# Two-input operations of GpSimd over more than 256 columns, issued in two halves

## The chip, the cores and the metric

The kernel runs on one core of a Trainium2 chip. Five engines work side by side, each through its own instructions in a fixed order: TensorE (PE; its weight loads are shown apart as PEld), VectorE (DVE), ScalarE (ACT), GpSimd (POOL) and SyncE (SP), which here issues the DMA transfers. They wait for each other through semaphores. The metric is the time of one execution on the device in microseconds (us). Three runs of the kernel before took 1324.07 to 1325.41 us, with a median of 1325.01 us.

## What is computed

One layer of a streaming encoder, for 2048 new frames with 16 meta tokens in front (the prompt) and for 32 new frames of a running stream with a cache of 528 rows (the sample). All numbers are float32. In short form:

```
n  = rmsnorm(x, norm_g)
q, k, v, z_a, b, c, u, z_c = split(n @ w_in, 8)          # 8 parts of 512 columns
# group A: differential attention, 4 heads, q and k in two halves of 64
s1, s2 = q1 k1 / 8 + bias, q2 k2 / 8 + bias              # chunk-causal, chunks of 64 frames
o  = (softmax(s1) - lam * softmax(s2)) @ v
o  = rmsnorm_per_head(o, subln_g) * 0.8 * silu(z_a)
# group B: gated short convolution
y  = silu(z_c) * b * conv3(c * u)                        # depthwise, causal, width 3
x  = x + concat(o, y) @ w_out
out = rmsnorm(x, final_g)
```

The outputs are the normalised rows of the prompt and the sample, the new keys and values, and the last two rows of the convolution's input.

## The kernel before

**Products in three parts.** TensorE multiplies in a reduced-precision form of float32. So each factor is split into a high part, rounded by a copy to that form, and a low part, the difference between the number and its high part. A product is the sum of high x high, high x low and low x high. The high parts are made by ScalarE (`S.copy`), the low parts by a subtraction with two inputs, which for the most part GpSimd does (`G.tensor_tensor(..., op=ALU.subtract)`) and for some tensors VectorE.

**Stages.** The prompt is worked on in four parts p of 512 frames; the first also carries the 16 meta tokens and the 32 sample frames, 560 columns in all. For each p, x is read transposed (`x_load`), scaled by norm_g and split into `xh` and `xl`; the normalising factor of each frame is kept in `rbs[p]` and applied to the results. For each of the four heads h follow:

- `unit_a(h, p)`: the projections q, k, v and z. `w_load` brings the 128 columns of one projection (`wr`), and splits them into `wh` and `wl` in two pieces of 4 x 128 columns (L196, L197). `proj` multiplies (L217): 24 matmuls for each block of 512 columns, or of 280, 272 or 288 for p = 0. The blocks are read out by VectorE with two inputs, PSUM and `rbs`. The low parts of q and k are made by GpSimd on 64 partitions (L252, L278), that of v on 128 (L313).
- `attend(h, p, st)`: for each row tile of 128 frames `softmax_diff` computes the scores of both halves in chunks of up to 512 columns (L438, L439), VectorE takes each row's extremum (L385, L388), and ScalarE the exponential (L389). `coefs` works out a few numbers per row on VectorE and ScalarE (L358 to L369), and each chunk is then combined by GpSimd, which scales the first half with one input (`G.tensor_scalar`, L392), and by VectorE, which adds the second half with two inputs (L393). TensorE transposes the result (L454), it is split again (L457, L458) and multiplied with v (L461 to L463). `post` normalises and gates it; its last product is GpSimd's (L422).
- `unit_c(u, p)`: the projections c, u, b and the gate with the convolution between them. GpSimd does three products here (L532, L554, L568).

Behind the four parts comes the output projection (`out_first`, `out_rest`), whose rows are split by `load_cat` (L664, L666) and whose weights by `w_half` (L649, L650), with matmuls at L686.

**The order of the work.** The program is written as loops, but the order of instructions on each engine is set by a scheduler, which simulates the engines with costs of its own as the kernel is built and takes what is ready by priority (`schedule_with_timeline_sim=True`). So the matmuls of one projection stand between those of another unit's attention. Where the code changes, the order is worked out again for all engines.

Of the kernel before, what the change touches and what calls it, by code (L numbers as in the profile page):

```python
# [13 lines left out]
AF = mybir.ActivationFunctionType  # L14
ALU = mybir.AluOpType
# [21 lines left out]
CQ, CK, CV, CZ, CB, CC, CU, CG = range(0, 32, 4)  # L37
# [10 lines left out]
def hybrid_step(ctx: ExitStack, tc: tile.TileContext, x, xT, ckT, cv, scT, rel_bias, norm_g, w_in,  # L48
# [10 lines left out]
    op = pool("op", 3)  # L59
# [9 lines left out]
    V, S, G, T = nc.vector, nc.scalar, nc.gpsimd, nc.tensor  # L69
    S.preload_act_table_set("natural_log_exp_and_others")  # L70
    f32 = lambda a: a.bitcast(F32) if a.dtype == F32R else a
    dma = lambda out, in_: nc.sync.dma_start(f32(out), f32(in_))
    g_tile = lambda n=564: gp.tile([P, 564], F32, tag="g", name="g")[:, :n]
    o_tile = lambda n=QT: op.tile([P, QT], F32, tag="o", name="o")[:, :n]
# [23 lines left out]
    rbs = {}  # L98
# [34 lines left out]
    def x_load(p):  # L133
        c0 = 0 if p == 0 else NX + QT * p
        tw = NX + QT if p == 0 else QT
        if p == 0:
            acc = [None, None]
        for k in range(KT):
            xt = g_tile(tw) if p == 0 else one.tile([P, QT], F32, tag="xt", name="xt", bufs=XB)
            dma(xt, xT[P * k:P * (k + 1), c0:c0 + tw])  # L140
            xh[k] = xp.tile([P, NX + QT], F32R, tag=f"xh{k}", name=f"xh{k}")
            xl[k] = xp.tile([P, NX + QT], F32R, tag=f"xl{k}", name=f"xl{k}")
            with tc.high_priority():
                S.activation(xh[k][:, :tw], xt, AF.Copy, scale=ng[:, k:k + 1])
                V.scalar_tensor_tensor(xl[k][:, :tw], xt, ng[:, k:k + 1], f32(xh[k][:, :tw]),  # L145
                                       op0=ALU.mult, op1=ALU.subtract)
            if p == 0:
                i = (1, 0, 1, 0, 1, 0, 0, 0)[k]
                sq = sqt(k, tw)
                (G.tensor_tensor(sq, xt, xt, op=ALU.mult) if i else S.activation(sq, xt, AF.Square))  # L150
                if acc[i] is None:
                    acc[i] = sq
                else:
                    (G if i else V).tensor_tensor(acc[i], acc[i], sq, op=ALU.add)
        if p == 0:
            rb = one.tile([P, NX + QT], F32, tag="rb", name="rb")
            for i in range(2):
                c = slice(280 * i, 280 * (i + 1))
                var, w = (pp.tile([P, 512], F32, tag="p1", name="xv", bufs=NP[1])[:, :280] for _ in range(2))
                ps = ps_t.tile([P, 2, 256], F32, tag="pt", name="pss").rearrange("p a b -> p (a b)")[:, :280]  # L160
                parts = [a[:, c] for a in acc if a is not None]
                for j, a in enumerate(parts):
                    T.matmul(ps, lhsT=ones, rhs=a, start=(j == 0), stop=(j == len(parts) - 1))
                with tc.high_priority():
                    rsqrt(rb[:, c], ps, var, w, 1.0 / D)
            rbs[0] = rb
# [21 lines left out]
    def w_load(col, p):  # L188
        wr = wp.tile([P, KT, P], F32, tag="wraw", name="wr")
        dma(wr, w_in[col])  # L190
        w2 = []
        for i in range(2):
            wh = wp.tile([P, KT // 2, P], F32R, tag="wh", name="wh", bufs=4)
            wl = wp.tile([P, KT // 2, P], F32R, tag="wl", name="wl", bufs=4)
            wi = wr[:, KT // 2 * i:KT // 2 * (i + 1)]
            S.copy(wh, wi)  # L196
            (V if (col in (CQ, CK) if p == 0 else col in (CQ, CZ)) else G).tensor_tensor(wl, wi, f32(wh), op=ALU.subtract)  # L197
            w2.append((wh, wl))
        return w2

# [28 lines left out]
    def unit_a(h, p):  # L229
# [8 lines left out]
        q32 = g_tile(tw)  # L238
# [6 lines left out]
        def ev_q(ps, b0, b1):  # L245
            V.scalar_tensor_tensor(q32[:, b0:b1], ps, -0.125, rbs[p][:, b0:b1], op0=ALU.mult, op1=ALU.mult)
            e = min(b1, f0 + QT)
            for c in range(2):
                r = slice(64 * c, 64 * c + 64)
                hi, lo = (t_[r, b0 - f0:e - f0] for t_ in qd[c])  # L250
                S.copy(hi, q32[r, b0:e])
                G.tensor_tensor(lo, q32[r, b0:e], f32(hi), op=ALU.subtract)  # L252
            if p == 0 and b1 == tw:
                for c in range(2):
                    V.tensor_copy(qs[64 * c:64 * c + 64, NS * c:NS * (c + 1)], q32[64 * c:64 * c + 64, smp])
        proj(CQ + h, p, ev_q)
        for c in range(2):
            r, o = slice(64 * c, 64 * c + 64), slice(64 - 64 * c, 128 - 64 * c)
# [6 lines left out]
        k32 = g_tile(tw)  # L265
        ks = [ks_tile(c) for c in range(2)]
# [4 lines left out]
        def ev_k(ps, b0, b1):  # L271
            V.tensor_tensor(k32[:, b0:b1], ps, rbs[p][:, b0:b1], op=ALU.mult)
            e = min(b1, kn)
            for c in range(2):
                r, o = slice(64 * c, 64 * c + 64), slice(64 - 64 * c, 128 - 64 * c)
                d = slice(k0 + b0, k0 + e)
                S.copy(ks[c][r, d], k32[r, b0:e])
                G.tensor_tensor(ks[c][o, d], k32[r, b0:e], f32(ks[c][r, d]), op=ALU.subtract)  # L278
        proj(CK + h, p, ev_k)
        dma(kT_p[h, :, k0:k0 + kn], k32[:, :kn])  # L280
        if p < NQ - 1:
# [17 lines left out]
        vh = kv.tile([P, 16, P], F32R, tag="vh", name="vh")  # L299
        vl = kv.tile([P, 16, P], F32R, tag="vl", name="vl")  # L300
# [9 lines left out]
        v32 = v32.rearrange("p (j d) -> p j d", d=P)  # L310
        S.copy(v32, pt)
        V.tensor_copy(vh[:, new], v32)
        G.tensor_tensor(vl[:, new], v32, f32(vh[:, new]), op=ALU.subtract)  # L313
        r0 = NM + QT * p
        dma(v_p[r0:r0 + QT, h].rearrange("(j q) d -> q j d", q=P), v32)
        if p < NQ - 1:
# [92 lines left out]
    def post(n, o32, sq, z, l1, dst):  # L409
        sqh, sql = (ap.tile([P, 2, 256], F32R, tag=t_, name="sqh").rearrange("p a b -> p (a b)")[:, :n]  # L410
                    for t_ in ("ah", "al"))
        V.tensor_copy(sqh, sq)
        V.tensor_tensor(sql, sq, f32(sqh), op=ALU.subtract)
        ps = ps_o.tile([P, 512], F32, tag="po", name="pss")[:, :n]
        T.matmul(ps, lhsT=ones_r, rhs=sqh, start=True, stop=False)
        T.matmul(ps, lhsT=ones_r, rhs=sql, start=False, stop=True)
        f = o_tile(n)
        S.activation(f, ps, AF.Ln, scale=1.0 / P, bias=leps[:, 0:1])
        V.scalar_tensor_tensor(f, f, 0.5, l1, op0=ALU.mult, op1=ALU.add)
        S.activation(f, f, AF.Exp, scale=-1.0)  # L420
        V.scalar_tensor_tensor(o32, o32, g2[:, 0:1], f, op0=ALU.mult, op1=ALU.mult)
        G.tensor_tensor(o32, o32, z, op=ALU.mult)  # L422
        dma(dst, by_tile(o32) if n == QT else o32)

    def attend(h, p, st):
# [93 lines left out]
    def unit_c(u, p):  # L519
# [9 lines left out]

        def ev_c(ps, b0, b1):  # L530
            V.tensor_tensor(c32[:, b0:b1], ps, rbs[p][:, b0:b1], op=ALU.mult)
            G.tensor_tensor(c32[:, b0:b1], c32[:, b0:b1], rbs[p][:, b0:b1], op=ALU.mult)  # L532
        proj(CC + u, p, ev_c)

        def spans(b0, b1):
# [15 lines left out]

        t4 = g_tile(tw)
        for s0, s1, off in spans(f0, tw):
            G.tensor_tensor(yc[:, s0 + off - 2:s1 + off - 2], yc[:, s0 + off - 2:s1 + off - 2], rbs[p][:, s0:s1],  # L554
                            op=ALU.mult)

        def ev_b(ps, b0, b1):
            for s0, s1, off in spans(b0, b1):
# [4 lines left out]
        def ev_g(ps, b0, b1):  # L563
            eb = e[:, b0:b1]
            V.tensor_tensor(zc[:, b0:b1], ps, rbs[p][:, b0:b1], op=ALU.mult)
            softplus_neg(eb, zc[:, b0:b1])
            S.activation(eb, eb, AF.Exp, scale=-1.0)
            G.tensor_tensor(zc[:, b0:b1], zc[:, b0:b1], t4[:, b0:b1], op=ALU.mult)  # L568
        proj(CG + u, p, ev_g)
        V.tensor_tensor(t4[:, f0:], zc[:, f0:], e[:, f0:], op=ALU.mult)  # L570
        dma(cat[p][:, :, 4 + u], by_tile(t4[:, f0:hn]))
# [81 lines left out]
    def load_cat(t, rows, spare=False):  # L653
        ct = wp.tile([P, KT, P], F32, tag="wraw", name="ct")
        dma(ct[:, :, :rows], cat_s if t == 16 else cat[t // 4][:, t % 4])
        parts = []
        for i in range(2):
            c = ct[:, 4 * i:4 * i + 4, :rows]
            if spare:
                chh, cll = [pp.tile([P, 4, P], F32R, tag="p0", name="cs", bufs=NP[0]) for _ in range(2)]  # L660
            else:
                chh = wp.tile([P, 4, P], F32R, tag="wh", name="chh", bufs=4)
                cll = wp.tile([P, 4, P], F32R, tag="wl", name="cll", bufs=4) if t < 16 else chh
            S.copy(chh[:, :, :rows], c)  # L664
            lo = cll[:, :, :rows] if t < 16 else cll[:, :, rows:2 * rows]
            (V if spare or t == 16 else G).tensor_tensor(lo, c, f32(chh[:, :, :rows]), op=ALU.subtract)  # L666
            parts.append((chh, cll))
        hi, lo = ([parts[k // 4][j][:, k % 4] for k in range(KT)] for j in range(2))
        return hi, lo if t < 16 else None
# [136 lines left out]
```

## Time and profile before

| | |
|---|---|
| runs before | 1324.07 to 1325.41 us, median 1325.01 us |
| the profiled execution | 1324.97 us, span 1323.2 us |
| TensorE busy | 1279.3 us, 97% of the span |
| VectorE busy | 1011.5 us, 76%, 2086 instructions |
| ScalarE busy | 738.0 us, 56% |
| GpSimd busy | 731.3 us, 55%, 659 instructions |
| granted TensorE clock, mean | 0.990 |

The span reaches from the first to the last instruction of the profiled execution. An engine counts as busy while one of its instructions runs, standing still inside an instruction included. L197 is line 197 of the kernel before. A row of a group gives line, engine, operation, written and read tiles, shape, count, then the busy time in us and the mean of one in ns, then the idle time of the engine just before these instructions and what ended it. A row of waits gives who waited for whom, the us in total, how often, and the longest. A row of the timeline gives start and length in us, and in brackets the idle time before.

### The profile page before, as it was taken

Reading aid. Unit: us, or ns where it says so; the run is one execution under the profiler, and the core shown is the slowest. Engines: PE = TensorE matmul, PEld = TensorE weight load, DVE = VectorE, ACT = ScalarE, POOL = GpSimd, SP = SyncE. Lnnn points to the kernel's source line nnn. Section 1 sums busy time; section 2 is a strip of 40 time slices with the busy share of each in tenths; the row PEclk is TensorE's granted clock in tenths of the full one; section 3 lists DMA queues with packets and bytes.
Section 4 is the critical chain, followed back from the end, with each engine's and each line's share of the span. In section 5 each row is a group of like instructions: output and inputs, shape, how many; then the busy total and the mean of one; then the engine's idle time right before and its main releaser. Section 6 shows DMA issues by size and latency. Waiting matters only on the chain.

```text
span 1323.2 us, 21113 instructions
## 1 busy us (share of the span) xinstructions
PE 1279.3 (97%) x7058; PEld 1102.2 (83%) x7058; DVE 1011.5 (76%) x2086; ACT 738.0 (56%) x1854; POOL 731.3 (55%) x659
## 2 busy tenths in 40 slices
PE   8999999999999998999999999999999999999997
PEld 6999899988788886888888788888888887888775
DVE  8766567668797857788878868888798898856754
ACT  6645453664665547566565466565656665654322
POOL 4665655656566664466556656466666575642200
PEclk9999999999999999899999999999999999999999
DMA  9744434674335356534253463344334534557752
GB/s 285 219 141 108 138 99 113 205 243 145 121 105 174 106 159 192 169 127 151 96 168 102 135 194 100 124 131 124 105 104 153 161 110 128 159 183 231 231 176 90
DMA packets 108046, 198.72 MB, mean 150 GB/s; under 512 B 17409, under 2 KB 45601, under 8 KB 107937
## 3 DMA queue, kind: packets, MB, share of 16 engines
q1 hardware_dynamic: 107936, 197.37, 48.4%
q8 instruction: 55, 0.90, 0.3%
q14 instruction: 55, 0.44, 0.1%
HBM read 145.62 MB, written 43.26 MB: 143 GB/s over the span
## 4 chain that ended last, share of the span: by engine, by line
PE 30%; DVE 12%; ACT 3%; issue 2%; POOL 2%; DMA 1%; DVEq 0%; POOLq 0%; ACTq 0%
PE po L686 10%; PE pj L217 10%; DVE p L393 4%; PE pt L454 2%; PE s L438 2%; DVE nm L388 2%; PE s L439 2%; ACT p L389 1%; PE po L462 1%; PE po L463 1%; PE po L461 1%; DVE al L458 1%; POOL wl L197 1%; PE po L678 1%; DMA out<-y 0%
## 5 line engine op out<-in xcount | busy, mean ns | idle before, releaser
L217 PE MATMUL pj<-xh,wh 128*128 128x512 f32 (+2 forms) x1280 | 457.0, 358 | 3.8 <-DVE g L344 1.0
L217 PE MATMUL pj<-xl,wh 128*128 128x512 f32 (+2 forms) x1280 | 455.2, 356 | 1.7 <-DVE xl L145 1.7
L197 POOL TENSOR_TENSOR wl<-wr,wh 128x512 fp32r<-128x512 f32 x240 | 327.7, 1370 | 232.5 <-ACT wh L196 220.6
L217 PE MATMUL pj<-xh,wl 128*128 128x512 f32 (+2 forms) x1280 | 453.5, 355 | 0.0
L389 ACT ACTIVATE p<-s,nm 128x384 f32<-128x384 f32 (+5 forms) x352 | 208.6, 595 | 164.5 <-DVE nm L388 126.0
L217 PEld LDWEIGHTS pj<-xh,wh 128*128 128x128 f32 x1280 | 243.3, 190 | 35.4 <-ACT bvec L596 1.7
L217 PEld LDWEIGHTS pj<-xl,wh 128*128 128x128 f32 x1280 | 242.9, 190 | 30.9 <-DVE xl L145 3.2
L217 PEld LDWEIGHTS pj<-xh,wl 128*128 128x128 f32 x1280 | 242.8, 190 | 30.0 <-issue 1.1
L196 ACT CAST wh<-wr 128x512 fp32r<-128x512 f32 x256 | 157.1, 617 | 99.6 <-PE pj L217 61.4
L393 DVE SCALAR_TENSOR_TENSOR p<-p,cf,p 128x384 f32<-128x384 f32 (+5 forms) x176 | 176.6, 1025 | 21.9 <-POOL p L392 21.2
L392 POOL TENSOR_SCALAR p<-p,cf 128x384 f32<-128x384 f32 (+5 forms) x176 | 122.1, 709 | 60.6 <-DVE cf L369 42.1
L438 PE MATMUL s<-ks,q 128*128 128x384 f32 (+5 forms) x352 | 130.1, 371 | 12.0 <-ACT p L389 11.8
L388 DVE TENSOR_REDUCE nm<-s 128x1 f32<-128x384 f32 (+3 forms) x224 | 121.8, 557 | 2.8 <-PE s L439 2.6
L439 PE MATMUL s<-ks,q 128*128 128x384 f32 (+5 forms) x352 | 123.7, 352 | 0.0
L458 DVE TENSOR_TENSOR al<-pt,ah 128x512 fp32r<-128x512 f32 x144 | 97.0, 681 | 34.6 <-ACT ah L457 34.5
L666 POOL TENSOR_TENSOR cll<-ct,chh 128x512 fp32r<-128x512 f32 x40 | 55.9, 1404 | 108.6 <-ACT chh L664 108.6
L457 ACT CAST ah<-pt 128x512 fp32r<-128x512 f32 x144 | 80.8, 586 | 39.1 <-PE pt L454 36.7
L454 PE MATMUL pt<-ident,p 128*128 128x128 f32 x544 | 88.4, 274 | 1.6 <-DVE p L393 1.4
L438 PEld LDWEIGHTS s<-ks,q 128*128 128x128 f32 x352 | 66.7, 189 | 25.8 <-ACT p L389 18.7
L462 PE MATMUL po<-al,vh 128*128 128x256 f32 x288 | 83.5, 290 | 2.1 <-DVE al L458 2.0
L461 PE MATMUL po<-ah,vh 128*128 128x256 f32 x288 | 81.3, 282 | 0.0
L463 PE MATMUL po<-ah,vl 128*128 128x256 f32 x288 | 81.2, 282 | 0.0
(238 smaller groups left out, 2214.4 us busy)
## 6 DMA issues: line engine op xcount, KB each, us to landing
wr<-in_w_in SPq DMA_DIRECT2D x128, 512.0 KB, 3.7
ct<-cat SPq DMA_DIRECT2D x28, 512.0 KB, 4.6
q<-q SPq DMA_DIRECT2D x64, 128.0 KB, 2.8
out<-y SPq DMA_DIRECT2D x32, 256.0 KB, 3.7
ks<-ksd SPq DMA_DIRECT2D x8, 776.0 KB, 5.2
xr<-in_x SPq DMA_DIRECT2D x24, 256.0 KB, 5.3
out<-g SPq DMA_DIRECT2D x24, 256.0 KB, 2.9
xt<-in_xT SPq DMA_DIRECT2D x24, 256.0 KB, 4.7
```

The costliest lines, as they stand in the source:

```text
L196: S.copy(wh, wi)
L197: (V if (col in (CQ, CK) if p == 0 else col in (CQ, CZ)) else G).tensor_tensor(wl, wi, f32(wh), op=ALU.subtract)
L217: T.matmul(ps, lhsT=a[:, k % 4], rhs=b[k][:, b0:b1], start=(k == 0 and i == 0), stop=(k == KT - 1 and i == 2))
L388: V.tensor_reduce(nm[:, c, j:j + 1], s, op=ALU.min, axis=AX.X)
L389: S.activation(pr[j][c], s, AF.Exp, bias=nm[:, c, j:j + 1], scale=-1.0, accum_out=l[:, c, j:j + 1])
L392: G.tensor_scalar(a0, a0, cf[:, 0, j:j + 1], 1.0, op0=ALU.mult, op1=ALU.mult)
L393: V.scalar_tensor_tensor(a0, a1, cf[:, 1, j:j + 1], a0, op0=ALU.mult, op1=ALU.add)
L438: T.matmul(ps, lhsT=qd[c][0][:, qs], rhs=ks[c][:, col:col + w], start=True, stop=False)
L439: T.matmul(ps, lhsT=qd[c][1][:, qs], rhs=ks[c][:, col:col + w], start=False, stop=True)
L454: T.transpose(pt[:, i, P * qi:P * (qi + 1)], cols(aa[qi], NM + P * (2 * j + i), P), ident)
L458: V.tensor_tensor(al, pt, f32(ah), op=ALU.subtract)
L686: T.matmul(ps, lhsT=a[k][:, :rows], rhs=b[k], start=(k == 0 and i == 0), stop=(k == KT - 1 and i == 2))
```

## The change

A function `halved` takes the place of `tensor_tensor` at ten places. Where the engine is GpSimd and the operation covers more than 256 columns (counted over all dimensions behind the partitions), it issues two instructions, one for each half of the first of these dimensions; otherwise one, as before. For VectorE, where a condition chooses it at L197 and L666, nothing changes. The operations with one input (L392), those of 32, 240 and 248 columns, and those of L154 and L650 stay as they are. 435 operations become 870 instructions.

```diff
+    def halved(out, a, b, op, engine=None):
+
+        n = out.shape[-1] if len(out.shape) == 2 else out.shape[1]
+        cuts = (0, n // 2, n) if engine is None and n * (out.shape[-1] if len(out.shape) > 2 else 1) > 256 else (0, n)
+        for c0, c1 in zip(cuts, cuts[1:]):
+            (engine or G).tensor_tensor(out[:, c0:c1], a[:, c0:c1], b[:, c0:c1], op=op)
...
-                (G.tensor_tensor(sq, xt, xt, op=ALU.mult) if i else S.activation(sq, xt, AF.Square))
+                (halved(sq, xt, xt, ALU.mult) if i else S.activation(sq, xt, AF.Square))
...
-            (V if (col in (CQ, CK) if p == 0 else col in (CQ, CZ)) else G).tensor_tensor(wl, wi, f32(wh), op=ALU.subtract)
+            halved(wl, wi, f32(wh), ALU.subtract, V if (col in (CQ, CK) if p == 0 else col in (CQ, CZ)) else None)
...
-                G.tensor_tensor(lo, q32[r, b0:e], f32(hi), op=ALU.subtract)
+                halved(lo, q32[r, b0:e], f32(hi), ALU.subtract)
...
-                G.tensor_tensor(ks[c][o, d], k32[r, b0:e], f32(ks[c][r, d]), op=ALU.subtract)
+                halved(ks[c][o, d], k32[r, b0:e], f32(ks[c][r, d]), ALU.subtract)
...
-        G.tensor_tensor(vl[:, new], v32, f32(vh[:, new]), op=ALU.subtract)
+        halved(vl[:, new], v32, f32(vh[:, new]), ALU.subtract)
...
-        G.tensor_tensor(o32, o32, z, op=ALU.mult)
+        halved(o32, o32, z, ALU.mult)
...
-            G.tensor_tensor(c32[:, b0:b1], c32[:, b0:b1], rbs[p][:, b0:b1], op=ALU.mult)
+            halved(c32[:, b0:b1], c32[:, b0:b1], rbs[p][:, b0:b1], ALU.mult)
...
-            G.tensor_tensor(yc[:, s0 + off - 2:s1 + off - 2], yc[:, s0 + off - 2:s1 + off - 2], rbs[p][:, s0:s1],
-                            op=ALU.mult)
+            halved(yc[:, s0 + off - 2:s1 + off - 2], yc[:, s0 + off - 2:s1 + off - 2], rbs[p][:, s0:s1], ALU.mult)
...
-            G.tensor_tensor(zc[:, b0:b1], zc[:, b0:b1], t4[:, b0:b1], op=ALU.mult)
+            halved(zc[:, b0:b1], zc[:, b0:b1], t4[:, b0:b1], ALU.mult)
...
-            (V if spare or t == 16 else G).tensor_tensor(lo, c, f32(chh[:, :, :rows]), op=ALU.subtract)
+            halved(lo, c, f32(chh[:, :, :rows]), ALU.subtract, V if spare or t == 16 else None)
```

The change also moves instructions. GpSimd, in the first head's attention (p = 0, h = 0), with `p` the tiles of the softmax chunks, `wl` a weight's low part and `g<-g,rb` the product at L532; first the order before, then the order of the change, whose line 78 is inside `halved` and whose L400 is the L392 of before:

```order
L392 TENSOR_SCALAR p_685<-p_685,cf 128x272
L197 TENSOR_TENSOR wl<-wr,wh 128x512
L392 TENSOR_SCALAR p_730<-p_730,cf 128x400
L532 TENSOR_TENSOR g<-g,rb 128x280
L197 TENSOR_TENSOR wl<-wr,wh 128x512
```

```order
L400 TENSOR_SCALAR p_697<-p_697,cf 128x272
L78 TENSOR_TENSOR wl<-wr,wh 128x256 x2
L78 TENSOR_TENSOR g<-g,rb 128x140 x2
L78 TENSOR_TENSOR wl<-wr,wh 128x256 x2
L400 TENSOR_SCALAR p_742<-p_742,cf 128x400
```

Each pair of halves stands together, with nothing of another kind between, and the scaling of the chunk of 400 columns now follows the product of L532 and another weight's low part. VectorE at the same place (`x` and `nm` are small tiles with a few numbers per row, ISA is L385's operation, `al` and `am` low parts), before and with the change, where L401 is L393, L396 is L388 and L393 is L385:

```order
L388 TENSOR_REDUCE nm<-s 128x1
L393 SCALAR_TENSOR_TENSOR p_730<-p_731,cf,p_730 128x400
L388 TENSOR_REDUCE nm<-s 128x1
L109 TENSOR_REDUCE x_2406<-ssq 128x4
L170 TENSOR_SCALAR x_2407<-x_2406 128x4
L385 ISA s,nm<-s,bz 128x256
L385 ISA nm 128x1
L458 TENSOR_TENSOR al<-pt,ah 128x512
L469 TENSOR_TENSOR am_116<-pm,am_116 16x256
```

```order
L396 TENSOR_REDUCE nm<-s 128x1
L181 TENSOR_TENSOR x_2475<-x_2474 128x4
L182 TENSOR_TENSOR x_2475<-x_2475,x_2473 128x4
L393 ISA s,nm<-s,bz 128x256
L393 ISA nm 128x1
L183 TENSOR_SCALAR x_2475<-x_2475 128x4
L466 TENSOR_TENSOR al<-pt,ah 128x512
L184 TENSOR_TENSOR x_2474<-x_2474,x_2475 128x4
L477 TENSOR_TENSOR am_116<-pm,am_116 16x256
L401 SCALAR_TENSOR_TENSOR p_742<-p_743,cf,p_742 128x400
```

The combining of the chunk of 400 columns stood between the two minima of L388; with the change it follows both of them, the small operations on `x`, one extremum with the bias, and the two splits `al` and `am`.

## The prediction

> **What bounds the kernel now.** I read the page first: its busy shares and its chain.
>
> ```profile
> span 1323.2 us, 21113 instructions
> PE 1279.3 (97%) x7058; PEld 1102.2 (83%) x7058; DVE 1011.5 (76%) x2086; ACT 738.0 (56%) x1854; POOL 731.3 (55%) x659
> PE 30%; DVE 12%; ACT 3%; issue 2%; POOL 2%; DMA 1%; DVEq 0%; POOLq 0%; ACTq 0%
> ```
>
> TensorE is busy 97% of the span, and the engine that the change touches is on 2% of the followed chain. So the question is what the remaining 43.9 us of TensorE idle time (1323.2 - 1279.3) are, and whether GpSimd has a hand in them. The busy time by stretch tells where they lie:
>
> ```profile
> 0.00:20.00 20.00, 14.18 (x48) 10.00 (x49) 14.59 (x24) 13.09 (x22) 9.28 (x16) 1.00 0.83 242
> 20.00:130.00 110.00, 109.26 (x832) 105.08 (x831) 79.13 (x216) 61.39 (x167) 68.07 (x71) 1.00 0.61 182
> 130.00:340.00 210.00, 201.98 (x1310) 182.62 (x1309) 144.53 (x314) 108.15 (x277) 125.24 (x117) 0.99 0.52 155
> 340.00:540.00 200.00, 192.49 (x957) 161.87 (x957) 155.25 (x329) 116.83 (x290) 119.35 (x103) 0.97 0.48 151
> 540.00:740.00 200.00, 196.71 (x1055) 169.20 (x1053) 170.26 (x348) 121.75 (x311) 117.06 (x105) 1.00 0.41 131
> 740.00:1040.00 300.00, 296.25 (x1553) 252.43 (x1552) 246.79 (x457) 182.27 (x439) 182.98 (x159) 1.00 0.43 129
> 1040.00:1180.00 140.00, 136.33 (x721) 115.69 (x720) 119.13 (x210) 86.93 (x221) 87.06 (x73) 1.00 0.45 145
> 1180.00:1300.00 120.00, 116.51 (x530) 92.96 (x530) 71.39 (x164) 42.90 (x115) 22.22 (x17) 0.99 0.65 207
> 1300.00:1323.20 23.20, 15.59 (x68) 12.33 (x66) 10.44 (x30) 4.72 (x16) 0.00 (x0) 0.90 0.14 51
> ```
>
> The columns are the stretch, its length, the busy time of TensorE, of its weight load, VectorE, ScalarE and GpSimd, then the granted clock. The first and last rows hold 5.8 and 7.6 us of idle TensorE (first loads, last output), which the change can't reach. The seven between them hold 30.5 us in all. Three of these also show a granted clock below 1.00: 1% of 210, 3% of 200 and 1% of 120 us, some 9 us of full clock lost. That is all there is to win: about 40 us. Then who ends these waits:
>
> ```profile
> PE s L438 <- ACT p L389: 11.8, 11, 3.3
> PE ptv L308 <- DVE g L297: 4.0, 3, 1.7
> PE pts L504 <- DVE as L499: 2.9, 2, 2.2
> PE po L462 <- DVE al L458: 2.0, 2, 1.3
> ```
>
> They are score matmuls waiting for a score tile to be read out (ScalarE's exponential at L389, which itself waits for VectorE's minimum at L388), or direct waits for VectorE. No row of this view names GpSimd. But GpSimd is behind VectorE's lateness in another way, which two pieces of the timeline show. Columns: start, length, engine, line. GpSimd, then VectorE:
>
> ```profile
> 656.47 1.61 POOL L568 TENSOR_TENSOR g<-g 128x512 f32<-128x512 f32 x1
> 658.04 1.74 POOL L197 TENSOR_TENSOR wl<-wr,wh 128x512 fp32r<-128x512 f32 x1
> 668.60 1.29 POOL L197 TENSOR_TENSOR wl<-wr,wh 128x512 fp32r<-128x512 f32 x1
> ```
>
> ```profile
> 656.85 1.78 DVE L419 SCALAR_TENSOR_TENSOR o<-o,g 128x512 f32<-128x512 f32 x1
> 668.80 1.11 DVE L363 TENSOR_TENSOR nm<-nm,M 128x8 f32<-128x8 f32 x1 [0.64 <-ACT p L389]
> ```
>
> L363 handles 8 columns and took 1.11 us: it began at 668.80, inside GpSimd's L197, and ended at 669.91, just after that instruction (669.89). L419 began inside L568, was still running when L568 ended at 658.08, and ended at 658.63; the next GpSimd instruction, already queued, took 1.74 instead of 1.29 us, longer by 0.45, about VectorE's turn. So a VectorE operation that needs what GpSimd holds stands still **until the end of GpSimd's whole instruction**, and gets its turn there, ahead of the next one. How much of that there is, from the groups by shape:
>
> ```profile
> L393 DVE SCALAR_TENSOR_TENSOR p<-p,cf,p 128x384 f32<-128x384 f32 x64 | 69.2, 1103 | 0.0
> L393 DVE SCALAR_TENSOR_TENSOR p<-p,cf,p 128x400 f32<-128x400 f32 x44 | 42.2, 958 | 14.2 <-POOL p L392 14.0
> L393 DVE SCALAR_TENSOR_TENSOR p<-p,cf,p 128x512 f32<-128x512 f32 x44 | 50.8, 1161 | 0.0
> L368 DVE TENSOR_TENSOR r<-r,lam 128x2 f32<-128x2 f32 x52 | 22.2, 427 | 1.4
> L367 DVE RECIPROCAL r<-M 128x2 f32<-128x2 f32 x52 | 8.5, 164 | 1.5
> ```
>
> ```profile
> 531.78 0.63 DVE L393 SCALAR_TENSOR_TENSOR p<-p,cf,p 128x400 f32<-128x400 f32 x1
> 661.19 0.73 DVE L393 SCALAR_TENSOR_TENSOR p<-p,cf,p 128x512 f32<-128x512 f32 x1
> ```
>
> Undisturbed, L393 takes 0.63 us at 400 columns and 0.73 at 512, by the line through these 0.615 at 384. Its three groups are longer by 64 x 0.49 + 44 x 0.33 + 44 x 0.43 = 65 us. L368, on the same two columns as L367 but with two inputs, is longer by 52 x 0.263 = 14 us. Doing the same for every VectorE instruction against the shortest tenth of its shape gives some 224 us standing: 203 us in 272 instructions behind GpSimd's two-input ones, 0.75 us each, and 21 us behind L392, which has one. A fifth of VectorE's 1011.5 busy us is this.
>
> The largest idle stretch of TensorE shows the link. TensorE, VectorE and GpSimd before it:
>
> ```profile
> 524.61 0.40 PE L217 MATMUL pj<-xh,wl 128*128 128x512 f32 x1
> 528.28 0.59 PE L438 MATMUL s<-ks,q 128*128 128x272 f32 x1 [3.28 <-ACT p L389]
> ```
>
> ```profile
> 523.85 1.24 DVE L363 TENSOR_TENSOR nm<-nm,M 128x4 f32<-128x4 f32 x1
> 525.61 1.22 DVE L173 TENSOR_TENSOR x<-x 128x4 f32<-128x4 f32 x1
> 526.95 0.57 DVE L388 TENSOR_REDUCE nm<-s 128x1 f32<-128x400 f32 x1
> ```
>
> ```profile
> 523.69 3.12 POOL L278 TENSOR_TENSOR ks<-g,ks 64x512 fp32r<-64x512 f32 x2 [0.19 <-ACT ks L277]
> 526.89 1.27 POOL L197 TENSOR_TENSOR wl<-wr,wh 128x512 fp32r<-128x512 f32 x1
> ```
>
> Two operations on four columns take 1.24 and 1.22 us behind the two instructions of L278, and the minimum at 526.95 that frees the score tile stands behind them. In the 6 us before the 33 TensorE gaps of over 0.2 us VectorE stood still 2.2 us in the mean, against 0.93 us in any 6 us (203 / 1310 x 6).
>
> **The change, part by part.** *Length of a half.* GpSimd's two-input operations by width:
>
> ```profile
> L197 POOL TENSOR_TENSOR wl<-wr,wh 128x512 fp32r<-128x512 f32 x240 | 327.7, 1370 | 232.5 <-ACT wh L196 220.6 <-PE pj L217 3.6 <-PE s L439 2.1
> L278 POOL TENSOR_TENSOR ks<-g,ks 64x280 fp32r<-64x280 f32 x8 | 6.2, 781 | 1.6 <-ACT ks L277 1.1
> L554 POOL TENSOR_TENSOR g<-g,rb 128x32 f32<-128x32 f32 x4 | 1.0, 243 | 0.0
> ```
>
> From 243 ns at 32 and 781 at 280 columns: 2.17 ns a column and 174 ns an instruction. This gives 1.28 us at 512 (the undisturbed 1.29 above) and 0.73 us at 256. Two halves are 1.46 us, 0.17 more. The lower bound is 0.13, since a following instruction starts some 0.04 us before its predecessor ends (658.04 against 658.08); the upper one 0.25, from the mean 1370 at 512 against 781 at 280, which has the waits in it. I take 0.17, the undisturbed rows. 435 operations are split (240 in L197, 40 in L666, 155 in the others), so GpSimd gets 435 x 0.17 = 74 us more, bounds 57 and 109: 55% busy becomes 61%. The cover is GpSimd's own idle time, 592 us, of which 220.6 before L197 wait for ScalarE's copy. If that cover fails, it is the slower rival below.
>
> *The standing of VectorE.* If VectorE gets its turn between halves, it waits for the rest of 0.73 instead of 1.29 us. 0.75 x 0.73 / 1.29 = 0.42 us; with GpSimd busier by a tenth about 300 such meetings, 127 us in place of 203. So VectorE wins some 75 us, and the bounds are 0 (no turn between the halves) and 100 (half of it). The 21 us behind L392 stay, since it isn't split.
>
> *From VectorE to TensorE.* VectorE runs ahead of or behind TensorE with idle time of its own; only what falls before the 30.5 us of gaps counts. If of the 2.2 us before each gap 45% go, and no gap shrinks by more than itself, 22 us go: the upper bound. Not every one of these waits is in the chain of the gap, and some gaps will have another cause behind the first. I take 12 us, four tenths of the 30.5. With fewer long gaps some of the 9 us of half clock go too; I take 2, bounds 0 and 4.
>
> *The order of the work.* The instruction order of every engine is worked out anew by the scheduler. The halves stand next to each other, but L392 and L393 come later in places, by up to some ten rows. The trace has no price for this; one gap like the largest quoted (3.28 us at 528.28) more, or one less, is the bound to either side, and I take 0.
>
> *Sum*, against the profiled execution's 1324.97 us, which is the median of 1325.01 within 0.04: 1325 - 12 - 2 = **1311 us**.
>
> **The rivals.** (1) *The gaps re-form.* VectorE is faster, but TensorE then waits at the next dependency, such as ScalarE, which waits often for VectorE and TensorE in turn. For it: TensorE is at 97% and the waits are spread over many lines. Against it: the rows above, in which VectorE stands in front of the gaps. 2 us remain: 1323 to 1326, and I put it at 1324.
>
> (2) *Slower: GpSimd comes late with L392.* Each pair of halves costs 0.17 us more and lets VectorE in between for some 0.45 us, so each split operation queued ahead of L392 delays it by about 0.6 us. VectorE already waits for it:
>
> ```profile
> DVE p L393 <- POOL p L392: 21.2, 32, 2.0
> ```
>
> There are 64 softmax tiles (16 row tiles, 4 heads). With one split operation ahead of each, L393 comes 64 x 0.6 = 38 us later in all, the transposes behind it too. If four in ten of that reach TensorE, 15 us, and the shorter waits give back only 9, the time is 1331. It decides from the point at which this row grows by more than VectorE wins, some 75 us, or at which half of it falls on tiles whose transposes are next on TensorE. Against it: 0.6 us is under what L197 waits for ScalarE each time.
>
> (3) *No turn between the halves*: the pair acts as one instruction of 1.46 us. VectorE's wait grows to 0.75 x 1.46 / 1.29 = 0.85 us, 27 us in all, a seventh more; the gaps grow alike, by 4 us: 1329. Against it stands 658.04, where GpSimd's next instruction, queued and ready, waited for VectorE. The Trainium skill, GPSIMD Engine Reference, section 2.1 Instruction dispatch, says that one GpSimd instruction's end doesn't hold back the next: each of its eight cores begins the next when its own share is done. By that rule there might be no moment in which all have let go; the trace has VectorE served in such a moment.
>
> **How the numbers follow.** The forecast has a chance of 0.64 and by itself runs from 1300 (22 and 4 us gone) to 1321 (a third of the 12). Rival 1 has 0.14, rival 2 has 0.16, rival 3 has 0.06. A measurement of this kernel tells about 0.2%, 2.65 us, from no change. Faster than that: the forecast and 0.02 of rival 1, 0.66. Within: 0.12 of rival 1 and 0.01 of rival 3, 0.13. Slower: rival 2 and 0.05 of rival 3, 0.21. The range of 8 in 10 takes the forecast's own and goes up to rival 2's price: 1300 to 1331.
>
> **What would show it.** Right: VectorE's busy time falls to 920 to 950 us with the same count of instructions, L368's mean from 427 to about 300 ns and L393's at 384 columns to about 0.9 us; GpSimd's rises to about 800 us with some 1094 instructions; a half of L197 lasts about 0.73 us when nothing disturbs it; TensorE's idle time between 20 us and the last 23 us falls from 30.5 to about 18. Wrong: L368's mean stays above 400 (rival 3); VectorE's falls but TensorE's idle time doesn't (rival 1); the wait of L393 for L392 goes beyond 60 us (rival 2). A long TensorE gap at a place that has none now would be the new order, which I priced at nothing.

## The result

The changed kernel takes 1297.1 us (median of 5 runs, 1293.76 to 1298.81) against 1325.41 us for the kernel before beside it (1324.07 to 1326.29): a ratio of 0.9783, 95% interval 0.9767 to 0.9799. It is faster by 28 us, twice the 14 us forecast, and just below the range of 1300 to 1331. The page of the changed kernel, span, busy shares and chain:

```profile
span 1297.0 us, 21616 instructions
PE 1269.9 (98%) x7058; PEld 1100.7 (85%) x7058; DVE 953.9 (74%) x2086; ACT 739.1 (57%) x1854; POOL 831.4 (64%) x1094
PE 53%; DVE 3%; DMA 3%; ACT 2%; POOL 2%; issue 1%; SPq 0%; DVEq 0%; POOLq 0%; ACTq 0%
```

VectorE runs the same 2086 instructions and is busy 57.6 us less (1011.5 before); GpSimd runs 435 more and is busy 100.1 us more (731.3 before). In the chain that ended last VectorE's share falls from 12% to 3%, and TensorE's grows from 30% to 53%. The stretches between first loads and last output, with the columns of the view of before:

```profile
20.00:130.00 110.00, 109.28 (x834) 105.33 (x833) 74.77 (x217) 61.46 (x167) 76.31 (x119) 1.00 0.62 182
130.00:340.00 210.00, 209.35 (x1374) 191.37 (x1373) 139.64 (x339) 115.41 (x297) 151.41 (x214) 1.00 0.53 160
340.00:540.00 200.00, 193.07 (x960) 162.29 (x960) 151.23 (x331) 117.83 (x292) 135.39 (x176) 0.97 0.51 155
540.00:740.00 200.00, 200.00 (x1076) 173.33 (x1075) 161.32 (x341) 121.00 (x304) 144.46 (x184) 1.00 0.42 133
740.00:1040.00 300.00, 298.85 (x1579) 256.75 (x1578) 239.52 (x471) 189.03 (x461) 205.29 (x260) 1.00 0.44 133
1040.00:1180.00 140.00, 138.80 (x740) 118.19 (x739) 103.90 (x193) 84.64 (x211) 88.18 (x103) 1.00 0.47 151
1180.00:1274.00 94.00, 90.60 (x393) 70.57 (x393) 58.91 (x146) 31.76 (x90) 18.57 (x22) 1.00 0.68 218
```

TensorE's idle time in these seven is 14.1 us (1254.00 - 1239.95), against 30.5. It is gone from 130 to 340 us (0.65 against 8.02) and from 540 to 740 us (0.00 against 3.29), and has hardly changed from 340 to 540 us (6.93 against 7.51). Two of the three stretches with a granted clock below 1.00 have it at 1.00 now. The mean clock of the execution, changed kernel and kernel before:

```profile
core 0: 1297.0 us, clock 0.994
```

```profile
core 0: 1323.2 us, clock 0.990
```

Who ends TensorE's waits now, in the order of the rows shown of before:

```profile
PE s L446 <- ACT p L397: 4.7, 3, 2.8
PE ptv L316 <- DVE g L305: 1.2, 1, 1.2
PE pts L512 <- DVE as L507: 0.4, 2, 0.3
PE po L470 <- DVE al L466: 0.7, 2, 0.3
```

They fall from 11.8, 4.0, 2.9 and 2.0 us. (Line numbers of the changed kernel are higher by 7 or 8: L446 is L438, L401 is L393, L400 is L392, L376 is L368.) VectorE's groups that told of the standing, GpSimd's halves of a weight's low part, and VectorE's wait for L392:

```profile
L401 DVE SCALAR_TENSOR_TENSOR p<-p,cf,p 128x384 f32<-128x384 f32 x64 | 57.3, 919 | 0.0
L376 DVE TENSOR_TENSOR r<-r,lam 128x2 f32<-128x2 f32 x52 | 16.1, 311 | 1.3
```

```profile
L78 POOL TENSOR_TENSOR wl<-wr,wh 128x256 fp32r<-128x256 f32 x480 | 384.7, 826 | 199.0 <-ACT wh L204 186.0 <-PE pj L225 4.5 <-PE s L446 1.8
```

```profile
DVE p L401 <- POOL p L400: 20.3, 31, 2.0
```

L368's mean goes from 427 to 311 ns, L393's at 384 columns from 1103 to 919. L368's shortest, middle and longest duration in ns, before and with the change (L376):

```profile
L368 DVE TENSOR_TENSOR r<-r,lam x52: 143/161/1273, 59.7 to 1169.7; 128x2 f32<-128x2 f32 x52
```

```profile
L376 DVE TENSOR_TENSOR r<-r,lam x52: 149/253/720, 60.8 to 1146.5; 128x2 f32<-128x2 f32 x52
```

The longest of these two-column operations was as long as a whole GpSimd instruction (1.29 us) and is now as long as a half (0.74 us). Read as before, instruction by instruction, VectorE stands 138 us in 344 instructions behind two-input operations of GpSimd (203 us in 272 before): 0.40 us each in place of 0.75. One such place, GpSimd in two pieces of the timeline and VectorE:

```profile
832.44 0.74 POOL L78 TENSOR_TENSOR wl<-wr,wh 128x256 fp32r<-128x256 f32 x1 [0.66 <-ACT wh L204]
...
833.14 1.19 POOL L78 TENSOR_TENSOR wl<-wr,wh 128x256 fp32r<-128x256 f32 x1
```

```profile
832.93 0.80 DVE L191 SCALAR_TENSOR_TENSOR g<-g 128x512 f32<-128x512 f32 x1
```

VectorE began inside the first half, which ended at 833.18, had its turn, and ended at 833.73; the second half, in the queue all the while, took 1.19 in place of 0.74 us, longer by 0.45 us, about VectorE's turn of 0.55.

### The profile page after: what moved, and what is told of

It is laid out like the page before. It is cut to its first block, busy times and chain, and to the rows that moved or that the text cites. A ratio compares the mean times of both kernels' runs of the same rounds, so it can differ in the third digit from the quotient of the medians.

```text
span 1297.0 us, 21616 instructions
## 1 busy us (share of the span) xinstructions
PE 1269.9 (98%) x7058; PEld 1100.7 (85%) x7058; DVE 953.9 (74%) x2086; ACT 739.1 (57%) x1854; POOL 831.4 (64%) x1094
## 4 chain that ended last, share of the span: by engine, by line
PE 53%; DVE 3%; DMA 3%; ACT 2%; POOL 2%; issue 1%; SPq 0%; DVEq 0%; POOLq 0%; ACTq 0%
PE pj L225 25%; PE po L693 9%; PE s L446 4%; PE s L447 3%; PE pt L462 3%; PE po L471 2%; PE po L470 2%; PE po L469 2%; DMA ct<-cat 1%; DMA out<-y 1%; PE po L685 1%; POOL cll L78 1%; DVE p L401 1%; DMA xt<-in_xT 0%; POOL wol L657 0%
## 5 line engine op out<-in xcount | busy, mean ns | idle before, releaser
L78 POOL TENSOR_TENSOR wl<-wr,wh 128x256 fp32r<-128x256 f32 x480 | 384.7, 826 | 199.0 <-ACT wh L204 186.0
L401 DVE SCALAR_TENSOR_TENSOR p<-p,cf,p 128x384 f32<-128x384 f32 (+5 forms) x176 | 155.8, 913 | 20.7 <-POOL p L400 20.3
L400 POOL TENSOR_SCALAR p<-p,cf 128x384 f32<-128x384 f32 (+5 forms) x176 | 123.4, 717 | 32.2 <-DVE cf L377 20.8
L78 POOL TENSOR_TENSOR cll<-ct,chh 128x256 fp32r<-128x256 f32 x80 | 66.7, 860 | 113.0 <-ACT chh L671 111.9
L396 DVE TENSOR_REDUCE nm<-s 128x1 f32<-128x384 f32 (+3 forms) x224 | 121.9, 558 | 17.2 <-PE s L447 16.9
L446 PE MATMUL s<-ks,q 128*128 128x384 f32 (+5 forms) x352 | 128.2, 366 | 4.8 <-ACT p L397 4.7
L393 DVE CUSTOM_DVE_ANT_0 s<-s,bz 128x512 f32<-128x512 f32 (+5 forms) x128 | 74.1, 588 | 15.1 <-PE s L447 12.2
```

What stands on the lines that cost most here:

```text
L78: (engine or G).tensor_tensor(out[:, c0:c1], a[:, c0:c1], b[:, c0:c1], op=op)
L396: V.tensor_reduce(nm[:, c, j:j + 1], s, op=ALU.min, axis=AX.X)
L400: G.tensor_scalar(a0, a0, cf[:, 0, j:j + 1], 1.0, op0=ALU.mult, op1=ALU.mult)
L401: V.scalar_tensor_tensor(a0, a1, cf[:, 1, j:j + 1], a0, op0=ALU.mult, op1=ALU.add)
L446: T.matmul(ps, lhsT=qd[c][0][:, qs], rhs=ks[c][:, col:col + w], start=True, stop=False)
```

## The experiments

The change does two things at once: it cuts instructions, and it makes the scheduler order all engines anew. **Theory A**: VectorE's shorter standing is the gain. **Theory B**: the new order is. For the first runs the cut is made behind the scheduler, in its finished list, so that every engine's order stays. The first piece keeps the waits, the last one the signal, so nothing that waits for the operation can start earlier by the signal of a first half. The edits of the runs are given in short form, not as they stand in the code:

```diff
+    for i in instructions:                       # after the scheduler, order unchanged
+        if not GpSimd two-input, or width <= 256, or L154 or L650: keep
+        for k, (c0, c1) in enumerate(zip(cuts, cuts[1:])):
+            piece(i, columns c0:c1, waits only if first, signal only if last)
```

The other way round, the changed kernel's list with the pairs joined again:

```diff
+    if GpSimd instruction and the one ahead of it are halves of one operation:
+        one instruction over both, the first one's waits, both signals
```

Two pairs with another instruction between them stay cut.

**Halves in the old order.**

```diff
-cuts = (0, n)
+cuts = (0, n // 2, n)          # behind the scheduler
```

> The kernel before with the same 435 operations in halves, but every engine's order left as it was before: only the instruction itself is cut, behind the scheduler. Theory A (VectorE's waiting for the end of a GpSimd instruction gets shorter, and that is the gain): 1300 us, between 1296 and 1306; VectorE's busy time near 955, L368's mean near 300 ns, TensorE's idle time between the first 20 and the last 23 us near 15 us. Theory B (the new order of the work is the gain): 1320 to 1326 us, TensorE's idle time near 30 us though VectorE's busy time falls.

1297.1 us (1296.37 to 1297.51), ratio 0.9794, 0.9780 to 0.9809: the time of the change itself. Its page, and the stretch from 20 us to the last 22 us:

```profile
PE 1267.5 (98%) x7058; PEld 1098.9 (85%) x7058; DVE 957.0 (74%) x2086; ACT 740.1 (57%) x1854; POOL 827.9 (64%) x1094
```

```profile
20.00:1273.00 1253.00, 1238.41 (x6946) 1077.00 (x6945) 932.83 (x2035) 722.55 (x1817) 816.05 (x1075) 1.00 0.50 154
```

TensorE's idle time there is 14.6 us. Theory A's numbers hold, but for L368's mean (346 ns, expected near 300), and the cut alone gives the whole gain. L368's longest is 718 ns.

**Whole operations in the new order.**

> The changed kernel with its new order on every engine, but 433 of its 435 pairs of halves joined to one instruction again. Theory A: 1320 to 1330 us, VectorE's busy time back at 1005 to 1020 us. Theory B: 1295 to 1302 us.

1314.7 us (1312.91 to 1315.12), ratio 0.9925, 0.9910 to 0.9940. Neither theory's range.

```profile
PE 1276.4 (97%) x7058; PEld 1101.2 (84%) x7058; DVE 1013.9 (77%) x2086; ACT 737.5 (56%) x1854; POOL 732.9 (56%) x661
```

```profile
20.00:1290.00 1270.00, 1247.04 (x6953) 1079.22 (x6952) 989.01 (x2034) 719.46 (x1816) 723.54 (x645) 0.99 0.49 152
```

VectorE is as busy as before, and stands 202 us; still TensorE is idle 23.0 us in place of 30.5. So the new order by itself is worth 10 us with whole operations, and nothing with halves. That both take away the same gaps is the likely reason, and not shown: from 540 to 740 us the idle time of 3.29 us falls to 1.16 with the new order and to 0.00 with the cut in the old one, but from 340 to 540 us it grows with the new order, from 7.51 to 9.19 us.

**A cut that hardly shortens the hold,** in the old order.

```diff
-cuts = (0, n)
+cuts = (0, n - 1, n)           # behind the scheduler
```

> The order of before, and each of the 435 operations cut into all columns but one, and one: as many instructions and as much added GpSimd time (435 x 0.17 = 74 us) as with halves, but GpSimd holds on to what VectorE waits for nearly as long as before. Theory A: VectorE's busy time stays at 1005 to 1030 us, 1325 to 1333 us; the excess over 1325 is what 74 us of GpSimd time cost. A variant, that the number of turns counts and not the length of the piece: 1300 to 1312 us.

1319.0 us (1318.22 to 1321.81), ratio 0.9962, 0.9949 to 0.9975: faster than before by 5 us, against both expectations. GpSimd's groups and the page:

```profile
L197 POOL TENSOR_TENSOR wl<-wr,wh 128x511 fp32r<-128x511 f32 x240 | 323.1, 1346 | 184.6 <-ACT wh L196 168.1 <-PE pj L217 8.0 <-ACT ah L457 2.5
L197 POOL TENSOR_TENSOR wl<-wr,wh 128x1 fp32r<-128x1 f32 x240 | 77.3, 322 | 0.0
```

VectorE stands 196 us and TensorE is idle 28.1 us. L368's longest is 1268 ns, as before. As many instructions as with halves, and 835 us of busy GpSimd, show no cost; but they bring about a fifth of the gain. It is the length of the hold that matters, and something small remains beside it.

**Four pieces, scheduled anew,** in `halved`.

```diff
-cuts = (0, n // 2, n) if ...
+cuts = tuple(n * k // 4 for k in range(5)) if ...
```

> The changed kernel with four pieces in place of two, scheduled anew. Theory A: the piece is 0.45 us in place of 0.73, so VectorE's standing falls again, from 138 to some 100 us, and GpSimd gets 435 x 2 x 0.17 = 148 us more, about 980 us busy; little idle TensorE time is left to win, so 1288 to 1298 us, unless GpSimd's length now counts: then 1298 to 1310. Theory B tells nothing but that the order is a third one: anywhere from 1295 to 1325.

1299.0 us (1295.29 to 1302.58), ratio 0.9800, 0.9778 to 0.9821. VectorE stands only 87 us, GpSimd is busy 982 us, and nothing is won beyond halves: the upper of the two ranges. L368's longest is 477 ns.

**Only the weights in halves, and all but the weights,** each in the old order.

```diff
-cut every two-input operation of GpSimd over 256 columns, but L154 and L650
+cut those of L197                          # weights only
+cut every one but L154, L197 and L650      # all but the weights
```

> The order of before, and only the 240 operations of L197 in halves. VectorE stands 116 of its 203 us behind these. Theory A, in proportion (27.5 us of time for 62 us of standing with all 435): standing falls by 36 us, 1324.6 - 16 = 1309 us. If the first microseconds saved count most, since the gaps run out: 1301 to 1306 us. If it is not the standing but the lone operations near the softmax (q, k, gates) that matter: above 1316 us.

> The order of before, and the other 195 operations in halves, L197 whole. VectorE stands some 82 us behind these. Theory A, in proportion: standing falls by 26 us, 1313 us. If the first microseconds saved count most: 1306 to 1311 us. The gains of this and of the run with the weights alone add up to 27.5 us if each gap has its own cause, and to more if the gaps run out.

1310.8 us (1308.93 to 1311.99), ratio 0.9886, 0.9871 to 0.9900; and 1309.2 us (1307.93 to 1309.97), ratio 0.9874, 0.9859 to 0.9888. The stretch between head and tail, of the one and the other:

```profile
20.00:1284.00 1264.00, 1242.95 (x6949) 1079.15 (x6948) 954.04 (x2035) 720.91 (x1817) 780.58 (x883) 0.99 0.49 152
```

```profile
20.00:1285.00 1265.00, 1245.62 (x6944) 1080.21 (x6943) 965.27 (x2037) 721.76 (x1818) 758.53 (x835) 0.99 0.49 152
```

Standing falls by 41 us (203 to 162) and by 26 us (203 to 177), the time by 15 and 17 us; together they would be 32, with both it is 27. So the gaps overlap a little, and the 195 other operations are worth more for each microsecond of standing than the 240 of the weights. 96 of them belong to the attention (L252, L278, L313 and L422); whether this is the reason is not shown. The weights alone follow theory A in proportion; the others go beyond it.

**Four pieces in the old order.**

```diff
-cuts = (0, n)
+cuts = (0, n // 4, n // 2, 3 * n // 4, n)      # behind the scheduler
```

> The order of before, all 435 operations in four pieces. Four pieces in a new order took VectorE's standing from 138 to 87 us and won nothing beyond halves. Theory F (TensorE's last 15 us of gaps have other causes, and what counts from here is not VectorE's standing): 1294 to 1300 us here too. Theory G (the order of that run was a bad one for it): 1285 to 1292 us.

1312.7 us (1307.9 to 1313.26), ratio 0.9893, 0.9873 to 0.9913: both theories of that expectation fall. Rows of its waits:

```profile
DVE p L393 <- POOL p L392: 67.1, 48, 5.5
...
PE pt L454 <- DVE p L393: 7.4, 7, 3.0
```

From two to four pieces VectorE's standing falls from 141 to 87 us, but its wait for L392, which stands behind the longer GpSimd work, grows from 30.4 to 67.1 us, and TensorE's transposes wait for L393 (1.4 us before the change). The new order of four pieces, in which this wait is 33.0 us, is 14 us faster. Against two pieces in the old order TensorE is idle 7.7 us more (22.3 against 14.6), and the granted clock is 0.991 in place of 0.997, some 8 us of 1311; the two come to about the 16 us. The transposes' 7.4 us are the part of this that the rows tie to L393, and so to the slower rival's mechanism. With two pieces in the old order its wait grew by 9 us (21.2 to 30.4) and the transposes' wait for L393 did not grow (0.5 us).

**The single column first,** in the old order.

```diff
-cuts = (0, n)
+cuts = (0, 1, n)               # behind the scheduler
```

> The order of before, the single column first, then all others. All columns but one, then one, was 5.6 us faster than before though VectorE stood nearly as long. If it is the second turn, soon after the first, that helps: no short piece follows the long one here, but one precedes it, so 1322 to 1327 us. If any second boundary helps, or if GpSimd being later helps: 1317 to 1321 us.

1318.6 us (1317.75 to 1320.69), ratio 0.9951, 0.9934 to 0.9967. VectorE stands 183 us. The place of the single column makes no difference that can be told, so it is not a second turn soon after the first.

**Three pieces, scheduled anew,** in `halved`. Where `n` counts four blocks of 128 columns, as for the weights, the pieces are 128, 128 and 256 columns.

```diff
-cuts = (0, n // 2, n) if ...
+cuts = (0, n // 3, 2 * n // 3, n) if ...
```

> The changed kernel with three pieces in place of two, scheduled anew. VectorE's standing between the 138 us of halves and the 87 us of quarters, near 108; GpSimd near 905 us busy. If standing still counts: 1290 to 1295 us. If what is won there is lost again in GpSimd's lateness, as with quarters: 1295 to 1301 us.

1291.6 us (1290.74 to 1292.69), ratio 0.9745, 0.9726 to 0.9764: 5 us below halves, their two intervals just apart, as expected if the standing still counts. No kernel here is faster.

```profile
PE 1266.6 (98%) x7058; PEld 1099.6 (85%) x7058; DVE 922.9 (72%) x2086; ACT 740.6 (57%) x1854; POOL 912.1 (71%) x1529
```

```profile
20.00:1267.00 1247.00, 1236.78 (x6938) 1077.09 (x6939) 897.23 (x2034) 722.77 (x1816) 898.29 (x1507) 1.00 0.49 154
```

TensorE's idle time is down to 10.2 us.

**Three pieces in the old order.** Here the columns are cut evenly everywhere.

```diff
-cuts = (0, n)
+cuts = (0, n // 3, 2 * n // 3, n)      # behind the scheduler
```

> The order of before, all 435 operations in three pieces. In a new order three pieces took 1291.6 us, 5 less than halves; four took 1299 us in a new order and 1313 in the old one, where L393 waited 67 us for L392. If the length of the piece made these 5 us: 1290 to 1296 us. If the new order is needed because GpSimd's added time makes L392 late in the old one: 1300 to 1306 us and a wait of L393 for L392 of 40 to 55 us.

1298.7 us (1297.63 to 1299.56), ratio 0.9806, 0.9791 to 0.9820; L393 waits 45.3 us for L392, in the new order 27.2. Between the two expectations, with the wait of the second: in the old order the shorter piece wins nothing over halves. As the pieces are not quite the same, the 7 us between the two orders are not the order's alone.

**The softmax's scaling and combining at a high priority**, with two and with four pieces.

```diff
-            G.tensor_scalar(a0, a0, cf[:, 0, j:j + 1], 1.0, op0=ALU.mult, op1=ALU.mult)
-            V.scalar_tensor_tensor(a0, a1, cf[:, 1, j:j + 1], a0, op0=ALU.mult, op1=ALU.add)
+            with tc.high_priority():
+                (the same two)
```

> The changed kernel with the scaling (L392 of before) and the combining (L393) of the softmax chunks at a high priority in the scheduler, so that they are queued ahead of other pieces. If what is left of the gaps comes from the wait of L393 for L392 (20 us in the changed kernel): 1288 to 1294 us. If these 20 us lie under TensorE's work: 1294 to 1301 us.

> Four pieces and the same priority. Four pieces had VectorE's standing at 87 us and the wait of L393 for L392 at 33 us (67 us in the order of before, at 1313 us). If this wait is what eats the gain of shorter pieces: 1284 to 1293 us. If GpSimd's 980 busy us are late everywhere (gates, q and k as well): 1296 to 1306 us.

1295.9 us (ratio 0.9782, 0.9766 to 0.9797) and 1303.5 us (0.9828, 0.9805 to 0.9850). The row that it should have moved, with two pieces:

```profile
DVE p L402 <- POOL p L401: 20.4, 30, 2.0
```

20.3 us without the priority; with four pieces 33.3 and 33.0. The edit did not make the wait for L392 shorter, so these two runs say nothing on what that wait costs.

**The row statistics of the next part one head earlier**, with two and with three pieces.

```diff
-            if h == 2 and p < NQ - 1:
+            if h == 1 and p < NQ - 1:
                 r = x_stats(p + 1)
```

> The changed kernel with the row statistics of the next part read one head earlier (h = 1 in place of 2). The longest gaps left in the changed kernel lie at 491 to 518 us, where the chain of small operations of these statistics stands in VectorE's queue ahead of the minima, with 10.2 us of half clock around them. If that chain makes the gaps: 1286 to 1293 us. If the gaps there come from the beginning of a new part in itself: 1294 to 1301 us.

> Three pieces, scheduled anew, and the row statistics one head earlier. With halves the latter took 2 to 3 us off and the half clock around 514 us from 10.2 to 3.4 us; with thirds that half clock is at 3.4 us already. If the two gains have different causes: 1287 to 1290 us. If the same: 1290 to 1294 us.

1294.6 us (0.9772, 0.9755 to 0.9788) and 1291.65 us (0.9749, 0.9732 to 0.9766). Neither can be told from its kernel without the edit. With two pieces the gaps at their place stay: 1.38 and 3.06 us (at 512.16 and 515.74), where they were 1.74 and 2.76 (at 514.09 and 517.67). So the statistics' chain alone does not make them.

**511 + 1 columns in the new order:** the pairs joined, and each then cut.

```diff
+cuts = (0, n - 1, n)           # behind the scheduler, on the joined list
```

> The changed kernel's order with its pairs joined, and each then cut into all columns but one, and one. In the old order this cut was 5.6 us faster than whole operations, with 7 us less standing; whole operations in this order took 1314.7 us. If the second boundary or GpSimd's later end is worth some microseconds by itself: 1307 to 1311 us. If the 5.6 us were an accident of the old order, like the 10 us between the two orders: 1312 to 1320 us.

1311.5 us (1310.41 to 1312.98), ratio 0.9904, 0.9888 to 0.9919, against 0.9925 (0.9910 to 0.9940) with whole operations, between the two expectations. The two intervals overlap. In the old order such cuts won 5 and 7 us by their ratios, here 3 that may be chance; which part of it is the few microseconds less of standing (7, 20 and 8) and which is GpSimd being later stays open.

In one table, with the standing of VectorE behind GpSimd's two-input operations, the wait of L393 for L392, and TensorE's idle time between 20 us and the last output. The kernel before took 1324.2 to 1326.2 us beside these runs, and the four with a priority or with earlier statistics are left out:

| kernel | time, us | standing | L393 for L392 | TensorE idle |
|---|---|---|---|---|
| before | 1325 | 203 | 21.2 | 30.5 |
| whole, new order | 1314.7 | 202 | 15.8 | 23.0 |
| 511 + 1, old order | 1319.0 | 196 | 24.9 | 28.1 |
| 1 + 511, old order | 1318.6 | 183 | 26.5 | 26.9 |
| 511 + 1, new order | 1311.5 | 194 | 16.7 | 22.5 |
| weights only | 1310.8 | 162 | 26.9 | 21.1 |
| all but weights | 1309.2 | 177 | 22.4 | 19.4 |
| halves, old order | 1297.1 | 141 | 30.4 | 14.6 |
| halves (the change) | 1297.1 | 138 | 20.3 | 14.1 |
| thirds, old order | 1298.7 | 108 | 45.3 | 15.5 |
| thirds | 1291.6 | 98 | 27.2 | 10.2 |
| quarters, old order | 1312.7 | 87 | 67.1 | 22.3 |
| quarters | 1299.0 | 87 | 33.0 | 14.3 |

## Why the prediction was right in kind and too small

*What bounds the kernel.* Right: the gaps of TensorE were behind VectorE's standing. With the order kept, the cut alone took the idle time from 30.5 to 14.6 us.

*Length of a half.* Right: 0.73 us forecast, 0.74 undisturbed (832.44). GpSimd's undisturbed time grew by some 80 us (435 x 0.19, two halves of 0.74 against 1.29), forecast 74; the rest of its 100 us is put down to more of VectorE's turns (344 in place of 272), which is not measured by itself. The upper bound of 0.25 us does not follow from the two rows named for it: a line through 781 ns at 280 and 1370 at 512 columns has a fixed part of only 0.07 us.

*The standing.* 76 us forecast, 65 measured (203 to 138), 0.42 us a meeting forecast, 0.40 measured; there were 344 meetings, not 300. So VectorE's busy time, 953.9 us, stayed just above the 920 to 950 named as a sign.

*From VectorE to TensorE.* This is the step that failed, in both of its terms. "I take 12 us, four tenths of the 30.5" was 16.4. "some of the 9 us of half clock go too; I take 2" was some 5: 1.0% of 1323.2 is 13.2 us of full clock lost before, 0.6% of 1297.0 is 7.8 now. I had cut the first down because "some gaps will have another cause behind the first", and the second without a reason. From 340 to 540 us the gaps did stay (6.93 us left of 7.51); but the stretches from 130 to 340 and from 540 to 740 us lost nearly all of theirs, and the half clock of the former with them.

*A term that was missing.* The span fell by 26.2 us: 16.4 us of idle time, 5.4 of clock, and about 4 more in which the profile calls TensorE busy. A matmul's row of 512 columns lasts 0.39 us while the next one starts 0.23 us later (508.93 and 509.16 in the changed kernel), so a gap of up to 0.16 us does not show as idle. Counted from the starts instead, each matmul's distance to the next beyond the median for its shape, outside half clock, comes to 25.0 us before and 19.4 with the change, over and above what shows as idle. That is 5.6 less, of the size of the 4; as the ends of matmuls are modelled, it is an estimate. "That is all there is to win: about 40 us" left such gaps out, and so the lower end of the range, 22 and 4 us below (1299, given as 1300), was too near. With the measured sizes the same sum gives 1325 - 16.4 - 5.4 - 4 = 1299, as it must for the profiled execution of 1298.81 us, the longest of the five; the median is 1297.1.

*The order.* "The trace has no price for this", and 0 with 3.3 us to either side: the order alone is worth 10 us with whole operations, three times that bound, and nothing with halves. The term came out right by luck: the bound I gave for it does not hold, and why the new order adds nothing to halves is not shown.

*The rivals.* The gaps did not re-form, except around 514 us, where they had been at 528. TensorE there:

```profile
514.09 0.59 PE L446 MATMUL s<-ks,q 128*128 128x272 f32 x1 [1.74 <-ACT p L397]
...
517.67 0.59 PE L446 MATMUL s<-ks,q 128*128 128x272 f32 x1 [2.76 <-ACT p L397]
```

The slower rival did not come with halves: L393's wait for L392 stayed at 20.3 us. With quarters in the old order its sign came, 67.1 us against the 60 named, and the time was 16 us longer than with halves there; its price had put 15 us on TensorE. A pair of halves without a turn between them is excluded by the row at 833.14. The Trainium skill, GPSIMD Engine Reference, section 2.1 Instruction dispatch, says that an instruction's end does not hold back the next. This did not keep VectorE from its turn here.

## What to carry to other kernels

An instruction that is far longer than its work (two columns in 0.43 us) is standing, and what it stands behind is read from whose end its own end follows; the remedy can be a shorter instruction on the *other* engine, even where that engine gets slower by it. How far to cut is a trade: the hold gets shorter with each piece, but each costs its fixed time, and work queued behind the pieces can get late. Here three pieces (in a new order) beat two and four; that lateness is what stops the gain at four is read from L393's wait, and was not tested by itself. When a scheduler reorders with the change, cut behind it once with the order kept: only that separates the edit from its order.

## What the runs showed of the hardware that was not expected

One column takes GpSimd 0.18 to 0.19 us when nothing disturbs it (0.32 in the mean, with the turns), as much as the 0.17 read off two widths. TensorE's short gaps cost more than themselves: where those from 130 to 340 us were gone, the granted clock there was 1.00 in place of 0.99. And GpSimd's time was free over a wide span: with 104 us more of it, in 511 + 1 columns, the kernel was not slower.
